# Recurrent stage of a hybrid decoder layer: the filler ordered between the first step's scores and its first inverse product, doubled

## The chip, the cores and the metric

One Trainium2 chip, of which the program uses one core. The metric is the device time of one execution in microseconds (us); of several runs the median stands. Five engines work side by side, each through its own queue in order: TensorE (PE in the profile; PEld is its weight loads), VectorE (DVE), ScalarE (ACT), GpSimd (POOL) and SyncE (SP, which here issues the DMAs). They wait for each other by semaphores.

## The reference

One layer over 2048 tokens of width 1024, all in float32: an RMSNorm, one input projection `p = h @ w_in` of 4224 columns, three branches on its columns, each with a SiLU gate, one output projection of the concatenated branches, the residual and a last RMSNorm.

- Branch A is differential attention: 4 heads, two causal softmax maps per head, `a = p0 - lam * p1`, and `a @ v`.
- Branch B is a short gated convolution of 256 channels.
- Branch C is the RWKV-7 recurrence, 4 heads of size 64. For each token

```
sa    = state @ kk_t
state = state * w_t - sa (kk_t * a_t)^T + v_t k_t^T
y_t   = state @ r_t
```

The kernel computes the recurrence in chunks of 64 tokens, which needs the inverse of a triangular 64x64 matrix for each chunk and head.

## The kernel before, in words

**Order of the work.** The 2048 tokens are two halves of 1024. A first stage projects what the recurrence of half 0 needs. Then four stages follow: `rwkv(0)`, `attention(0)`, `rwkv(1)`, `attention(1)` (lines 1420 to 1431), and at the end what is left of the filler. The order on TensorE is the order in which the program text issues its products; the other engines and the DMA queue are ordered by a scheduler that follows the program's order and an estimate of times.

**Filler.** All other products are one long list, the generator `filler` (line 1287): input projections of the convolution, of the attention heads and of half 1's recurrence, and at its end the output projection. An input projection (`inproj`, line 348) takes one weight tile of 128 columns through two chunks of 512 tokens, 24 products (line 357) per chunk, since float32 is done in three products of split operands. The weight tile is loaded by SP into one buffer (`fetch_w`, line 324) and split into a high and a low part by POOL (`load_w`, lines 341 and 343), with two buffers each. A chunk ends with its evacuation by ScalarE and DVE (lines 462 to 480 for the convolution, 374 to 408 for attention) and mostly a store. Between the two halves the list also rebuilds the normalized input (`stats`, line 224, and `make_h1`, line 305), while `attention(0)` runs.

The output projection comes as 16 output tiles of 48 products each (`out_tile`, line 1238; the product is line 1254). Tile i may start only when `state["allowed"]` is over i: it is 8 at first, and line 1428 raises it to 10, 12, 14 and 16 as the pairs of the last head of `attention(1)` are finished. If the next tile isn't allowed, `pull` (line 1318) gives nothing.

**How filler gets into a stage.** A stage is a generator too. Where it has issued something whose result takes a while, it yields a hint in microseconds, and `run` (line 1340) answers with filler until the hint is used up, at 0.216 per product (`T512`); hints are scaled by `SCALE`, 1.0 for `rwkv(0)` and 0.92 for `rwkv(1)`:

```
for f in gen:
    state["owed"] = max(state["owed"], -OWE) + f * scale
    while state["owed"] > 0:
        if not pull():
            state["owed"] = 0.0
            break
```

**The recurrent stage.** `rwkv(half)` (line 487) goes through a half in four steps of 256 tokens. A step has three parts. `early` (line 520) loads the projected rows, computes decay and gate inputs (the products of lines 533, 537, 564, 582 and 587, with a normalizing factor that goes through POOL at lines 572 and 577). `scores` (line 594) computes the chunk's score blocks (line 617), sends their triangular 16x16 blocks through DRAM into another layout (lines 638 and 640) and calls `inverse` (line 679), which inverts them on DVE (lines 693 and 696), stores them (`zd`, line 700) and loads them back as diagonal blocks (`Z`, line 703, eight DMAs). `late` (line 705) transposes these blocks on DVE (X, line 718), and its first product is the first inverse product, line 726; further inverse products and the state's update follow. After the first step's `early` and `scores` have been issued, each `late` is woven together with `early` and `scores` of the next step (lines 860 to 893). Line 870 stands once per half, between the first step's scores and its `late`:

```
for f in chain(0):
    if f != "free":
        yield f
yield WAIT[0]
for n in groups:
    lt, nx = late(st[n]), chain(n + 1)
```

**Attention.** A score unit is a pair of products (lines 1006 and 1007), a maximum on DVE (line 1012) and an exponential on ScalarE (line 1015); after each unit `attention` yields a hint (line 1191). Weighing (lines 1042 and 1052), transposes (line 1082), their copies (line 1087) and the products with V (line 1074) are spread between the units.

Of the kernel before, what the change touches and what calls it, by code (L numbers as in the profile page):

```python
# [61 lines left out]
LAG = 2  # L62
OSC = 1
PS = ((1, 0), (1, 1, 1, 1))
WAIT = (8.0, 15.0)
XH = 0.3
HC = 2.656
HG = 2.047
# [76 lines left out]
def trunk(ctx, tc, a, o, phases="RTO"):  # L145
# [341 lines left out]
    def rwkv(half, pool):  # L487
# [379 lines left out]
# [5 lines that stand above are left out]
# [15 lines left out]
            while more:  # L887
# [3 lines left out]
                elif x != "free":  # L891
                    yield x
            yield WAIT[1]

# [585 lines left out]
```

## Time and profile before

| what | value |
|---|---|
| time, median of 3 runs | 1620.57 us (1619.04 to 1622.68) |
| the profiled execution, its own time | 1626.87 us |
| its span, from the first instruction to the last | 1625.1 us |
| mean granted clock of TensorE in it | 0.965 of full speed |
| busy: PE, DVE, ACT, POOL | 93%, 55%, 44%, 40% of the span |
| TensorE instructions | 10328 |

All rows of the profile come from one execution, so they are to be read against its own time. A row of the timeline gives the start in us from the span's start, the duration, engine, line and operation, what is written and read, the number of equal instructions merged in it, and in brackets the idle time of the engine just before it and the instruction that ended it. Products are pipelined: each is shown for about 0.4 us, while the next starts 0.23 us later. The granted clock is 1.00 at 2.4 GHz and 0.50 at 1.2 GHz, and a mean between the two in a stretch that has both.

### The profile page before, as it was taken

The numbers are of one execution on the slowest core, as the hardware profiler recorded it, in microseconds if no ns is written. First come the engines' busy times: TensorE is split into PE (matmuls) and PEld (weight loads), VectorE is DVE, ScalarE is ACT, GpSimd is POOL, SyncE is SP. The second block draws the span as 40 slices with busy tenths as digits, with TensorE's granted clock in tenths as the row PEclk, the third lists the DMA queues.
The fourth block names the chain that finished last, engine by engine and source line by source line (L and its number), as shares of the span: only waits on it lengthen the run. The fifth ranks groups of instructions, "written<-read, shape, count | busy, mean of one in ns | idle before, by whom it ended". The sixth has DMA issues, their size and how long they took to land.

```text
span 1625.1 us, 28369 instructions
## 1 busy us (share of the span) xinstructions
PE 1512.6 (93%) x10328; PEld 1224.4 (75%) x10328; DVE 891.0 (55%) x1987; ACT 720.3 (44%) x1751; POOL 649.1 (40%) x898
## 2 busy tenths in 40 slices
PE   5999899999997879999989999999899999988998
PEld 4777677878786657888867878788678878766886
DVE  7553555554215766862545565427757756775611
ACT  6432121222126555652212212127668777776732
POOL 4675334352325543434432434333534323111343
PEclk9999899999999989999979999999999999988999
DMA  6324212233376543323323222263544243321233
GB/s 220 104 91 160 67 33 80 73 102 100 116 246 203 149 145 117 103 73 128 112 72 101 74 56 61 70 220 97 152 129 157 93 143 100 95 77 40 67 111 110
DMA packets 140620, 180.76 MB, mean 111 GB/s; under 512 B 34336, under 2 KB 85568, under 8 KB 140480
## 3 DMA queue, kind: packets, MB, share of 16 engines
q1 hardware_dynamic: 140480, 178.94, 35.3%
q8 instruction: 82, 1.34, 0.4%
q14 instruction: 58, 0.48, 0.1%
HBM read 125.40 MB, written 53.48 MB: 110 GB/s over the span
## 4 chain that ended last, share of the span: by engine, by line
PE 71%; DVE 8%; issue 4%; DMA 3%; ACT 3%; POOL 3%; SPq 1%; POOLq 0%; DVEq 0%; ACTq 0%
PE pj L357 33%; PE ops L1254 10%; PE av L1074 7%; PE aT L1082 4%; PE S L1006 3%; PE S L1007 3%; DVE nm L1012 1%; DVE P L1052 1%; ACT P L1042 1%; ACT P L1015 1%; DVE tmpx L693 1%; PE G L617 1%; PE wu L770 1%; POOL wl L343 1%; PE chp L814 1%
## 5 line engine op out<-in xcount | busy, mean ns | idle before, releaser
L357 PE MATMUL pj<-hh,wh 128*128 128x512 f32 x1008 | 414.1, 411 | 7.9 <-DVE tlo L394 3.8
L357 PE MATMUL pj<-hh,wl 128*128 128x512 f32 x1008 | 412.9, 410 | 0.1
L357 PE MATMUL pj<-hl,wh 128*128 128x512 f32 x1008 | 409.9, 407 | 0.0
L343 POOL TENSOR_TENSOR wl<-wr,wh 128x256 fp32r<-128x256 f32 x324 | 261.6, 837 | 46.7 <-ACT wh L338 43.5
L1015 ACT ACTIVATE P<-S,nm 128x512 f32<-128x512 f32 (+3 forms) x320 | 199.5, 625 | 99.9 <-DVE nm L1012 89.2
L1012 DVE TENSOR_REDUCE nm<-S 128x1 f32<-128x512 f32 (+3 forms) x320 | 192.8, 607 | 88.8 <-PE S L1007 84.5
L357 PEld LDWEIGHTS pj<-hh,wh 128*128 128x128 f32 x1008 | 192.5, 191 | 50.5 <-issue 10.3
L357 PEld LDWEIGHTS pj<-hh,wl 128*128 128x128 f32 x1008 | 192.4, 191 | 42.8 <-issue 3.3
L357 PEld LDWEIGHTS pj<-hl,wh 128*128 128x128 f32 x1008 | 192.8, 191 | 38.9 <-issue 1.4
L341 POOL TENSOR_SCALAR wh<-wr 128x512 fp32r<-128x512 f32 x132 | 83.6, 650 | 272.3 <-PE pj L357 202.7
L1006 PE MATMUL S<-K,QH 128*128 128x512 f32 (+2 forms) x320 | 129.6, 405 | 31.8 <-ACT P L1015 31.6
L1074 PE MATMUL av<-aTf,V 128*128 128x256 f32 x576 | 152.8, 390 | 0.5 <-ACT aTf L1087 0.5
L1007 PE MATMUL S<-K,QL 128*128 128x512 f32 (+2 forms) x320 | 120.5, 377 | 0.0
L1052 DVE SCALAR_TENSOR_TENSOR P<-P,sc 128x512 f32<-128x512 f32 (+3 forms) x160 | 112.1, 735 | 13.2 <-ACT P L1042 9.5
L1074 PEld LDWEIGHTS av<-aTf,V 128*128 128x128 f32 x576 | 104.3, 196 | 12.2 <-ACT aTf L1087 1.1
L1254 PE MATMUL ops<-woh,wh 128*128 128x512 f32 x256 | 105.6, 413 | 5.6 <-ACT wh L1233 5.6
L1087 ACT COPY aTf<-aT 128x512 f32<-128x512 f32 x144 | 83.5, 584 | 56.7 <-PE aT L1082 55.9
L1254 PE MATMUL ops<-wol,wh 128*128 128x512 f32 x256 | 106.0, 414 | 0.0
L1254 PE MATMUL ops<-woh,wl 128*128 128x512 f32 x256 | 105.9, 414 | 0.0
L1011 DVE TENSOR_TENSOR S<-S,bt 128x256 f32<-128x256 f32 (+1 forms) x152 | 57.6, 379 | 84.1 <-PE S L1007 78.2
L1006 PEld LDWEIGHTS S<-K,QH 128*128 128x128 f32 x320 | 62.9, 196 | 53.2 <-ACT P L1015 40.4
L1082 PE MATMUL aT<-con,P 128*128 128x128 f32 x576 | 92.2, 285 | 11.3 <-DVE P L1052 8.3
(289 smaller groups left out, 2323.9 us busy)
## 6 DMA issues: line engine op xcount, KB each, us to landing
wr<-in_wt_dram SPq DMA_DIRECT2D x81, 512.0 KB, 3.8
wr<-mx SPq DMA_DIRECT2D x128, 64.0 KB, 2.0
oxt<-in_x_dram SPq DMA_DIRECT2D x32, 256.0 KB, 3.1
out_dram<-oxt SPq DMA_DIRECT2D x32, 256.0 KB, 2.4
prw<-s SPq DMA_DIRECT2D x28, 256.0 KB, 2.0
V<-pv SPq DMA_DIRECT2D x24, 256.0 KB, 2.9
x<-in_xT_dram SPq DMA_DIRECT2D x16, 256.0 KB, 6.3
pv<-t SPq DMA_DIRECT2D x16, 256.0 KB, 2.3
```

The lines of the kernel that those rows point to most:

```text
L341: nc.gpsimd.tensor_scalar(wh[:, ks], wr[:, ks], 1.0, 1.0, ALU.mult, ALU.mult)
L343: nc.gpsimd.tensor_tensor(wl[:, ks], wr[:, ks], wh[:, ks].bitcast(F32), ALU.subtract)
L357: mm(ps, lhs[:, k], rhs[c][k], start=(n == 0), stop=(n == 3 * NK - 1))
L1006: mm(s[:, 0:sw], QH[:, m, off:off + P], K[:, m, 0:sw], start=True, stop=False)
L1007: mm(s[:, 0:sw], QL[:, m, off:off + P], K[:, m, 0:sw], start=False, stop=True)
L1012: nc.vector.tensor_reduce(nm[:, m, g:g + 1], s[:, 0:gw], AX.X, ALU.max, negate=True)
L1015: act(p[:, 0:gw], s[:, 0:gw], AF.Exp, bias=nm[:, m, g:g + 1], accum_out=l[:, m, g:g + 1])
L1052: stt(pt[1, g][:, 0:gw], pt[1, g][:, 0:gw], sc[:, 1, g:g + 1], pt[0, g][:, 0:gw], ALU.mult, ALU.add)
L1074: mm(av[:, 0:256], Vs.get((h, kc))[:, ko:ko + P], tf[:, d * 256:d * 256 + 256], start=kb + d == 0, stop=kb + d == nb - 1)
L1082: nc.tensor.transpose(t[:, d * 256 + qi * P:d * 256 + qi * P + P], x["A"][g][:, ko:ko + P], ident)
L1087: cpy(tf, t)
L1254: mm(ps, l[:, k], Ws[n][r][k], start=(c == 0), stop=(c == 3 * NK - 1))
```

## The change

The first of the two values of `WAIT` is 16 in place of 8. It is read at line 870 alone, once in `rwkv(0)` and once in `rwkv(1)`; the second value (line 893, after each step's `late`) stays. No instruction is added or taken away.

```diff
 LAG = 2
 OSC = 1
 PS = ((1, 0), (1, 1, 1, 1))
-WAIT = (8.0, 15.0)
+WAIT = (16.0, 15.0)
 XH = 0.3
 HC = 2.656
 HG = 2.047
```

## Rows read from the trace of the kernel before

**Rows 1.** The page: busy time, share of the span and instructions of the engines.

```profile
PE 1512.6 (93%) x10328; PEld 1224.4 (75%) x10328; DVE 891.0 (55%) x1987; ACT 720.3 (44%) x1751; POOL 649.1 (40%) x898
```

**Rows 2.** What TensorE waited for, whole span: us in total, times, longest.

```profile
PE S L1006 <- ACT P L1015: 31.6, 17, 6.6
PE p L726 <- DVE X L718: 16.0, 3, 7.9
```

**Rows 3.** Timeline of TensorE at the first step of half 0.

```profile
190.76 0.39 PE L357 MATMUL pj<-hh,wh 128*128 128x512 f32 x1
190.99 0.40 PE L357 MATMUL pj<-hl,wh 128*128 128x512 f32 x1
199.30 1.05 PE L726 MATMUL p<-X,N 32*32 32x16 f32 x64 [7.91 <-DVE X L718]
...
211.72 0.95 PE L564 MATMUL ssp<-conr,e 128*128 128x2 f32 x8
```

**Rows 4.** Timeline of TensorE at the first step of half 1.

```profile
812.09 0.40 PE L357 MATMUL pj<-hh,wl 128*128 128x512 f32 x1
819.69 1.05 PE L726 MATMUL p<-X,N 32*32 32x16 f32 x64 [7.20 <-DVE X L718]
...
832.25 0.95 PE L564 MATMUL ssp<-conr,e 128*128 128x2 f32 x8
```

**Rows 5.** Stretches: length, busy per engine (instructions), granted clock, DMA share, GB/s.

```profile
199.30:204.00 4.70, 4.70 (x72) 3.08 (x72) 1.05 (x3) 0.84 (x2) 0.00 (x0) 0.50 0.43 152
...
208.00:212.00 4.00, 4.00 (x76) 3.36 (x74) 2.95 (x6) 0.73 (x2) 1.87 (x2) 0.65 0.19 66
212.00:216.00 4.00, 4.00 (x50) 3.19 (x51) 0.46 (x2) 0.95 (x2) 2.42 (x3) 1.00 0.02 4
```

**Rows 6.** Timeline of TensorE at the second step of half 0.

```profile
269.21 0.72 PE L726 MATMUL p<-X,N 32*32 32x16 f32 x64 [0.94 <-DVE X L718]
...
276.74 0.95 PE L564 MATMUL ssp<-conr,e 128*128 128x2 f32 x8
...
284.39 0.81 PE L582 MATMUL bcp<-con,e__2679 128*128 128x128 f32 x4 [2.29 <-POOL e__2679 L577]
```

**Rows 7.** Timeline of all engines between inverse and X, half 0.

```profile
192.17 0.32 SPq L700 DMA_DIRECT2D zd<-Zs  x1
...
193.00 0.69 DVE L479 SCALAR_TENSOR_TENSOR th<-th,pj 128x512 f32<-128x512 f32 x1 [1.32 <-ACT th L478]
193.71 3.63 SPq L703 DMA_DIRECT2D Z<-zd  x8
...
198.71 0.45 DVE L718 STREAM_TRANSPOSE X<-Z 128x256 f32<-128x256 f32 x1 [5.02 <-DMA Z<-zd]
```

**Rows 8.** Timeline of POOL: casts of the next weight tile, half 0 and half 1.

```profile
179.30 2.82 POOL L343 TENSOR_TENSOR wl<-wr,wh 128x256 fp32r<-128x256 f32 x4
...
798.01 2.82 POOL L343 TENSOR_TENSOR wl<-wr,wh 128x256 fp32r<-128x256 f32 x4
```

**Rows 9.** Line 1254 alone by stretches: length, TensorE busy (products), clock, DMA share, GB/s.

```profile
1230.00:1414.50 184.50, 109.17 (x372) 1.00 0.35 109
1414.50:1491.00 76.50, 0.48 (x1) 0.89 0.23 68
...
1574.60:1618.00 43.40, 43.40 (x189) 1.00 0.37 119
```

**Rows 10.** ScalarE by line, from 1230 to 1414.5 and from 1414.5 to 1491.

```profile
L1015 ACT ACTIVATE P<-S,nm 128x512 f32<-128x512 f32 (+3 forms) x90 | 57.8, 642 | 22.8 <-DVE nm L1012 21.2 <-DVE ors L1112 1.0
...
L1015 ACT ACTIVATE P<-S,nm 128x512 f32<-128x512 f32 (+3 forms) x46 | 29.8, 649 | 5.4 <-DVE nm L1012 5.0 <-DVE mn L1026 0.3
```

**Rows 11.** Stretches before and in the hold, columns as in rows 5.

```profile
1384.00:1414.50 30.50, 30.50 (x155) 25.66 (x153) 21.63 (x54) 21.04 (x55) 6.42 (x10) 1.00 0.19 59
1414.50:1491.00 76.50, 64.46 (x311) 52.54 (x309) 56.15 (x140) 61.93 (x158) 8.55 (x14) 0.89 0.23 68
```

**Rows 12.** Timeline of POOL ahead of line 582, second step of half 0.

```profile
282.19 1.65 POOL L572 TENSOR_TENSOR rn<-ssb,mexp 128x8 f32<-128x8 f32 x1
```

**Rows 13.** The stretch of the input's rebuilding in the first attention, columns as in rows 5.

```profile
480.00:630.00 150.00, 120.92 (x549) 97.02 (x548) 102.10 (x242) 86.50 (x235) 71.10 (x98) 0.91 0.54 167
```

## Prediction
> **What bounds the kernel now.** I read the page's shares first: TensorE is busy for 1512.6 us of the 1625.1 us span [rows 1], in an order of its own written out by the program, so time is lost where it stands idle or runs slowly. The list of what TensorE waits for comes next [rows 2]. Two lines lead it. One is spread over attention (17 waits for the exponentials of ScalarE); the other, 16.0 us in three waits, is the first inverse product (line 726) waiting for the transposed blocks X (line 718), which is the place that the change touches.
>
> The timeline shows two of these three waits to be the first step of each half. In half 0 the last filler product before it starts at 190.99 us; products follow each other at 0.23 us, so TensorE is free at 191.22, and the inverse product starts at 199.30 after an idle time of 7.91 us [rows 3]. In half 1 the same happens from 812.09 to 819.69, with 7.20 us idle [rows 4]. The stall costs more than itself: behind half 0's the granted clock is 0.50, the 1.2 GHz level, still 0.65 in the mean from 208 to 212 us, and 1.00 (2.4 GHz) from 212 [rows 5]. What that costs can be read by comparison. From the inverse product to the product of line 564 the program issues the same list in each of these steps, filler included. Half 0's first step needs 211.72 - 199.30 = 12.42 us for it, half 1's 832.25 - 819.69 = 12.56 us, and half 0's second step, which came from a wait of only 0.94 us and was not slowed, 276.74 - 269.21 = 7.53 us [rows 3, 4, 6]. So the low clock costs 4.9 and 5.0 us.
>
> **The change, part by part.** It raises one hint from 8 to 16. A hint is turned into filler at 0.216 per product and is scaled by 1.0 in half 0 and by 0.92 in half 1: 8 / 0.216 = 37 more products before the first inverse product of half 0, 7.36 / 0.216 = 34 in half 1. Nothing is added or removed in the kernel; 71 products with what hangs on them come earlier.
>
> *At the stall.* 37 x 0.23 = 8.5 us end at 191.22 + 8.5 = 199.7, 34 x 0.23 = 7.8 us end at 812.32 + 7.8 = 820.1. X would have let TensorE go at 199.30 and 819.69, so each inverse product starts 0.4 us later than now, without an idle time ahead of it, and what follows runs at the 2.4 GHz level: 0.4 - 4.9 = -4.5 us and 0.4 - 5.0 = -4.6 us, together **-9.1 us** by the end of the second recurrence, with 71 products done that are still to come in the kernel before.
>
> Does X come as it does now? Its chain is DVE, ScalarE, a store (192.17), eight loads on SP (from 193.71, 3.63 us) and the transpose at 198.71 [rows 7]; none of it hangs on filler. The 37 and 34 products are less than one weight tile of 48, whose weights POOL had cast by 182.1 and 800.8 us [rows 8]; in half 0 a tile had just ended. The casts of the tile after that come from one tile further on, beside the stall in both kernels. The new filler ends one 24-product group in front of X; its evacuation (one ScalarE and one DVE operation, DVE's like the 0.69 us of the one at 193.00 [rows 7]) can come between the loads and X on DVE, which I bound at 0 to 0.7 us in each half and take at 0, since X is only needed at the end of the filler. SP gets one store of 256 KB at most, behind the eight loads in program order. I put it at nothing; if it slipped ahead it would cost one issue, by the eight loads 3.63 / 8 = 0.45 us.
>
> *Where the 71 products are missing.* Not in the last stretch. The filler ends in output tiles of 48 products, and the program lets only tiles 0 to 7 go before the last head's first pair is finished. In the trace these 8 x 48 run out at 1414.5 us; between 1414.5 and 1491 there is one such product in the record, and attention goes on bare [rows 9]. Tile 8 starts with that pair in both kernels, so the 189 products of the pure tail stay. What changes is that the bare stretch begins 71 products earlier. With filler, 184.5 us carry 90 score units, 2.05 us each with 372 / 90 = 4.1 products; bare, 76.5 us carry 46, 1.66 us each [rows 9, 10]. 71 / 4.1 = 17 units become bare, at 2.05 - 1.66 = 0.39 us: **-6.7 us**. The bounds are from the same rows. Above: a unit costs as much bare as filled, 0. Below: all of their 71 x 0.23 = 16.3 us comes off. In the 30.5 us before the hold TensorE is busy throughout and ScalarE for 21.0 us [rows 11], so the lower bound would need ScalarE to do nearly all of that in 14.2 us; the hold's mean is the nearest row.
>
> The clock is where a rule speaks against this part. The hold has a granted clock of 0.89 where the stretches before have 1.00 [rows 11]. The Trainium skill, "TensorE: Matmul & The Clock Gate", section "A second HAM failure mode: psum-queue depth-cycling", says that short idle times between groups of products can keep the clock swinging between its levels, so that throughput falls without any one long wait; by it a longer bare stretch would be worth nothing, and the sum would be -9.1 us. The trace agrees as far as 0.89 goes, and the 1.66 us already hold it.
>
> **The sum** is -9.1 - 6.7 = -15.8 us. In the profiled execution's own time, 1626.87 us, that is 1611.1; that execution lies 6.3 us above the median of 1620.57, against which I state it: 1620.57 - 15.8 = **1604.8 us**.
>
> **The rivals.**
> (a) The hold takes all of it back: -9.1 us, 1611.5. For it speaks its low clock, against it the 1.66 us.
> (b) The 71 products come off whole: -9.1 - 16.3 = -25.4 us, 1595.2. Against it ScalarE's 21.0 us.
> (c) The filler meets other work. Every later transfer of the filler falls 37 or 71 products earlier against recurrence and attention. A weight cast or a gating product on POOL just ahead of the chain to line 582 is such a meeting: in the second step it held POOL until 282.19, and TensorE waited 2.29 us [rows 6, 12]. More is at stake in the first attention, where the filler rebuilds the normalized input for half 1: 480 to 630 us holds 150 - 120.9 = 29.1 us of idle time at a clock of 0.91 [rows 13]. If that grew by half, 14.5 us, the result would be -1.3 us, 1619.3; it can as well shrink. From about 19 us more it would be slower.
> (d) Slower: X slides behind the new filler. If the inverse chain, its loads or the transpose were ordered after the added evacuations, on DVE or SP, the old wait would stand behind 8.5 and 7.8 us of more filler, with the low clock behind it: +16.3 - 6.7 = +9.6 us, 1630.2. With the low clock back the front is at +0.8 plus the new waits, so with the hold's 6.7 us it decides from 5.9 us of new waits over both halves. Against it: SP issues the loads 1.2 us after the store, with no filler's transfer between [rows 7].
> (e) The hints do nothing (the filler held or used up): 1620.6. The filler isn't held before the output tiles, so this is nearly excluded.
>
> **How the numbers follow.** Forecast 0.58, with a range of its own from 1599 to 1611 (collisions on POOL and shifts in the handover, each a few us either way); (a) 0.16; (b) 0.08; (c) 0.11; (d) 0.05; (e) 0.02. A measurement of this kernel can tell about 0.2%, 3.2 us, from no change. Faster: 0.58 + 0.16 + 0.08 and 0.04 of (c) = 0.86. Same: 0.06 of (c) and (e) = 0.08. Slower: (d) and 0.01 of (c) = 0.06. The range reaches to (b) below and past (a) above, to 1616, which takes in 4.5 us of collisions beside (a); outside are (d), (e) and most of (c).
>
> **What would show it.** Right: the two long waits of line 726 for X gone, or under 1 us; the granted clock 1.00 through both first steps; from the inverse product to line 564 some 7.5 us in each; the second recurrence's end about 9 us earlier with 71 products more behind it; the last output product before the hold about 17 x 2.05 + 9.1 = 44 us earlier than 1414.5, the hold some 17 units longer, and as many products in the pure tail. Wrong: a wait of over 3 us left at line 726, a hold whose units cost 2 us, or an idle time between 480 and 630 us that differs from 29 us by more than 8.

## The result, and the profile after

| what | before | after |
|---|---|---|
| median (lowest to highest) of 4 runs, us | 1620.46 (1619.04 to 1622.68) | 1604.62 (1603.98 to 1606.58) |
| ratio, 95% interval | | 0.9892, [0.9870, 0.9914] |
| profiled execution: own time, span, us | 1626.87, 1625.1 | 1604.13, 1601.9 |
| mean granted clock | 0.965 | 0.977 |

The changed kernel is 15.8 us faster. The page's first part answers to [rows 1]: TensorE is busy for 12 us less, and its share of the span goes up from 93 to 94%.

```profile
PE 1500.6 (94%) x10328; PEld 1213.6 (76%) x10328; DVE 894.2 (56%) x1987; ACT 722.1 (45%) x1751; POOL 645.9 (40%) x898
```

The list of TensorE's waits over the whole span (us in total, times, longest) answers to [rows 2]. The wait for X has gone from 16.0 us to 3.2, and second stands a projection's product (line 357) that waits 8.1 us in one piece.

```profile
PE S L1006 <- ACT P L1015: 30.2, 19, 5.2
PE pj L357 <- DVE tlo L394: 8.1, 1, 8.1
...
PE p L726 <- DVE X L718: 3.2, 3, 1.5
```

The timeline of TensorE shows the two places of [rows 3, 4] (start, duration, in brackets the idle time ahead and who ended it), between them the product that waits 8.15 us, and last the end of the stretch without filler, the first product of output tile 8.

```profile
200.24 0.73 PE L726 MATMUL p<-X,N 32*32 32x16 f32 x64
...
207.78 0.95 PE L564 MATMUL ssp<-conr,e 128*128 128x2 f32 x8
...
477.46 0.77 PE L357 MATMUL pj<-hh,wh 128*128 128x512 f32 x1 [8.15 <-DVE tlo L394]
...
814.95 0.72 PE L726 MATMUL p<-X,N 32*32 32x16 f32 x64 [1.51 <-DVE X L718]
...
822.24 0.95 PE L564 MATMUL ssp<-conr,e 128*128 128x2 f32 x8
...
1472.03 0.80 PE L1254 MATMUL ops<-woh,wh 128*128 128x512 f32 x1 [5.73 <-ACT wh L1233]
```

The wait at 477.46 is not new as such. The same product (1440 of line 357 go before it in both kernels) waits in the kernel before too, but less, and later. There 1406 of these products stand ahead of the first attention's first score, so it falls inside attention. The change puts 1443 ahead of that score, and the wait moves in front of attention. Timeline of the kernel before, whose first score is at 478.5 us:

```profile
494.63 0.76 PE L357 MATMUL pj<-hh,wh 128*128 128x512 f32 x1 [3.79 <-DVE tlo L394]
```

In half 0 there is no wait left for X, and line 564 follows 7.54 us behind the inverse product; in half 1 a wait of 1.51 us is left, and it is 7.29 us. Before it was 12.42 and 12.56. The stretches (columns as in [rows 5]) say why: the clock behind the inverse product is 1.00 where it was 0.50.

```profile
200.20:204.00 3.80, 3.77 (x76) 2.45 (x75) 1.38 (x3) 0.84 (x2) 0.00 (x0) 1.00 0.55 197
815.00:819.00 4.00, 3.96 (x76) 2.68 (x77) 1.68 (x3) 0.84 (x2) 0.00 (x0) 1.00 0.51 184
1370.00:1471.00 101.00, 81.37 (x396) 64.68 (x394) 75.23 (x189) 80.28 (x209) 11.63 (x19) 0.92 0.20 59
480.00:630.00 150.00, 124.82 (x593) 102.10 (x593) 108.17 (x255) 84.58 (x226) 73.56 (x101) 0.92 0.47 148
```

The third of these lines is the bare stretch, which answers to [rows 11]. From its last output product (1369.38 us) to the next one (1472.03) it is 102.6 us long, where the kernel before has 80.5 us in its profile and 77.1 in a second one (run e6 below). ScalarE's line for it (as [rows 10]) holds 62 score units, 16 more than before:

```profile
L1015 ACT ACTIVATE P<-S,nm 128x512 f32<-128x512 f32 (+3 forms) x62 | 40.1, 649 | 9.8 <-DVE nm L1012 9.3 <-DVE mn L1026 0.3
```

**Where the time went, by stage.** I cut each kernel's TensorE timeline at the same instructions: the first score block of a half (line 617), line 564 of its first step, line 833 of its fourth step, and the first and last scores of attention (line 1006). "Handover" is from a recurrence's fourth step to the first attention score. Since the profiled execution of before lay 6.3 us above the median, the kernel before was profiled a second time (the run e6 below, 1620.91 us). The two differ mainly in the first attention, 234.1 against 228.2 us. I take that for scatter between executions. The differences in this text go by the second profile, and each other stage time comes from one profile too, so a few us in the first attention say little.

| stage, us | before | before, second | after | difference |
|---|---|---|---|---|
| first step, half 0 | 43.7 | 44.6 | 39.4 | -5.2 |
| steps 2 to 4 | 214.2 | 213.3 | 209.4 | -3.9 |
| handover | 52.6 | 52.5 | 61.7 | +9.2 |
| attention, half 0 | 234.1 | 228.2 | 226.9 | -1.3 |
| first step, half 1 | 42.2 | 42.2 | 38.9 | -3.3 |
| steps 2 to 4 | 203.0 | 203.0 | 202.3 | -0.7 |
| handover | 48.6 | 48.6 | 50.6 | +2.0 |
| attention, half 1, up to the last tiles | 411.3 | 411.2 | 396.9 | -14.3 |
| last tiles | 122.7 | 122.5 | 122.6 | +0.1 |

What is not in the table differs by 0.3 us at most. The spans differ by -17.2 us, against -15.8 by the medians.

### The profile page after: what moved, and what is told of

Same layout as the page of the kernel before. It is cut to its first block, busy times and chain, and to the rows that moved or that the text cites. A ratio compares the mean times of both kernels' runs of the same rounds, so it can differ in the third digit from the quotient of the medians.

```text
span 1601.9 us, 28378 instructions
## 1 busy us (share of the span) xinstructions
PE 1500.6 (94%) x10328; PEld 1213.6 (76%) x10328; DVE 894.2 (56%) x1987; ACT 722.1 (45%) x1751; POOL 645.9 (40%) x898
## 4 chain that ended last, share of the span: by engine, by line
PE 68%; DVE 8%; DMA 5%; ACT 4%; issue 3%; SPq 3%; POOL 2%; DVEq 0%; POOLq 0%; ACTq 0%
PE pj L357 31%; PE ops L1254 10%; PE av L1074 7%; PE S L1006 3%; PE aT L1082 3%; PE S L1007 3%; ACT P L1042 1%; ACT P L1015 1%; DVE nm L1012 1%; PE wu L770 1%; PE G L617 1%; DMA wr<-in_wt_dram 1%; POOL wl L343 1%; DMA xt<-in_x_dram 1%; DVE P L1052 1%
## 5 line engine op out<-in xcount | busy, mean ns | idle before, releaser
L357 PE MATMUL pj<-hh,wl 128*128 128x512 f32 x1008 | 407.4, 404 | 0.6 <-POOL wl L343 0.5
L1082 PE MATMUL aT<-con,P 128*128 128x128 f32 x576 | 91.4, 283 | 14.9 <-DVE P L1052 7.8
```

The costliest lines, as they stand in the source:

```text
L357: mm(ps, lhs[:, k], rhs[c][k], start=(n == 0), stop=(n == 3 * NK - 1))
L1082: nc.tensor.transpose(t[:, d * 256 + qi * P:d * 256 + qi * P + P], x["A"][g][:, ko:ko + P], ident)
```

## The experiments

None of these kernels leaves out any part of the computation; they only order the same work differently. Edits are against the changed kernel. Each was compared with the kernel before on its own chip, and the ratios are to that.

### One half at a time

`e1_half0`:

```diff
-        yield WAIT[0]
+        yield (16.0, 8.0)[half]
```

> 16 in half 0, 8 kept in half 1. Theory (cover): the wait of line 726 in half 0 is gone and its low clock with it (-4.5 us), and 37 products fewer stand beside the second attention ahead of the hold (9 units bare, at 0.39 to 0.65 us: -3.5 to -5.9): 1610 to 1613 us, half 1's wait of 7 us unchanged. Rival (handover): what half 0 gains is taken back where half 1's input is rebuilt, as the new wait of 8.1 us for tlo at 477 us of the changed kernel suggests: within 3 us of the kernel before.

Measured: 1609.63 us, ratio 0.9932 [0.9911, 0.9953]. Its timeline:

```profile
200.79 0.72 PE L726 MATMUL p<-X,N 32*32 32x16 f32 x64
...
476.38 0.77 PE L357 MATMUL pj<-hh,wh 128*128 128x512 f32 x1 [6.67 <-DVE tlo L394]
...
812.33 1.05 PE L726 MATMUL p<-X,N 32*32 32x16 f32 x64 [8.90 <-DVE X L718]
```

`e2_half1`:

```diff
-        yield WAIT[0]
+        yield (8.0, 16.0)[half]
```

> 8 in half 0, 16 in half 1. Theory (cover): half 0's wait of 7.9 us stays, half 1's goes with its low clock (-3.3 to -4.6 us, since X came 1.5 us late in the changed kernel), and 34 products fewer ahead of the hold (-3.2 to -5.3): 1611 to 1614 us, and both halves alone add up to the whole change. Rival (handover takes half 0's share back): nearly the whole gain is here, 1605 to 1608.

Measured: 1620.77 us, 0.9986 [0.9967, 1.0005]. Its timeline in half 1:

```profile
813.28 0.73 PE L726 MATMUL p<-X,N 32*32 32x16 f32 x64 [0.56 <-DVE X L718]
...
820.60 0.95 PE L564 MATMUL ssp<-conr,e 128*128 128x2 f32 x8
```

Each half's wait goes with its own hint, and only with that: 5.1 us less in the first step of half 0 in e1, 4.0 us less in that of half 1 in e2. The wait in the first handover comes with half 0's hint. Half 0's part is worth 0.7%. Half 1's part alone gives no measurable gain, against the 1611 to 1614 us that was expected, so the two do not add up to the whole. In e2's profile what the front wins is lost in the same half: steps 2 to 4 take 206.9 us for 203.0. Of that 1.4 us is idle time (with new waits of 2.47 us at line 357 and 1.44 us at line 582), the rest busy time of TensorE at a granted clock of 0.98 for 0.99.

### The same filler, but not earlier as a whole

`e3_moved_within` gives 8 us back behind the last step, so the front is filled and no product leaves attention for the recurrence:

```diff
-            yield WAIT[1]
+            yield WAIT[1] - (8.0 if n == len(groups) - 1 else 0.0)
```

> 16 at the first step and 8 less after the last step of each half, so that the 71 products come from within the stage and the hold begins where it did before. Theory (cover): 15.1 us of waits and 9.9 us of low clock come off, less 0.8 us, and the 71 products removed elsewhere are off a busy TensorE: -24 us, 1596, about 8 us faster than the changed kernel. Rival (handover): with 8 us less between the stages the second half's input and the attention's first loads come too late, and 5 to 10 us are given back there: 1602 to 1608.

Measured: 1598.86 us, 0.9863 [0.9841, 0.9885], which is lower than the changed kernel's 0.9892, though the two intervals overlap. Its profiled execution (1593.87 us) is 5.0 us below its median. The fronts are as in the changed kernel (39.4 and 38.0 us). The second attention takes 410.8 us up to the last tiles, as before. What it wins beside the front is in the handovers, 43.9 and 40.8 us for 52.5 and 48.6, for the filler that is taken out there; the first attention is 3.6 us longer (231.8 us for 228.2), which is within the scatter seen above.

`e5_late_only` is the opposite: the kernel before, with the 8 us added behind the last step.

```diff
-WAIT = (16.0, 15.0)
+WAIT = (8.0, 15.0)
...
-            yield WAIT[1]
+            yield WAIT[1] + (8.0 if n == len(groups) - 1 else 0.0)
```

> 8 kept at the first step, and 8 more after the last step of each half: the same 71 products earlier, but not where the stall is. Theory (cover): both waits of line 726 and the low clock stay; 16.3 us of products more in the stages, of which the hold gives back 6.7 (by the prediction) to 10.4 us (by the two traces): 6 to 10 us slower than the kernel before, 1626 to 1630. Rival (position): the gain comes from the filler being ahead, whatever it covers: faster than before, 1605 to 1615.

Measured: 1619.24 us, 0.9982 [0.9968, 0.9996], between the two ranges expected. Both waits and the low clock behind them stay:

```profile
200.58 1.05 PE L726 MATMUL p<-X,N 32*32 32x16 f32 x64 [7.82 <-DVE X L718]
...
825.34 1.05 PE L726 MATMUL p<-X,N 32*32 32x16 f32 x64 [8.93 <-DVE X L718]
...
836.72 0.95 PE L564 MATMUL ssp<-conr,e 128*128 128x2 f32 x8
```

Against the second profile of before, the handovers grow by 14.3 and 8.3 us and the first attention shrinks by 5.6. The second attention up to the last tiles shrinks by 16.5 us, as it does by 14.3 us in the changed kernel. Sending these 71 products ahead of attention is worth about 15 us there, whichever hint sends them; the place where they are put then decides whether that is kept.

### More, and less, of it

`e4_24` and `e7_12` change the one number (24.0 and 12.0 for 16.0 in line 65).

> 24 in place of 16: another 37 and 34 products with no wait left to cover. Theory (stall covered at 16, products ahead of the hold come off at nearly their own price, as the late-only run showed): 16.3 us more in the stages, 14 to 19 us less in the second attention, so within 4 us of the changed kernel, 1601 to 1609, no wait at line 726. The prediction's own sizing of the hold (6.7 us back for 71 products): 9.6 us slower than the changed kernel, 1614.

Measured: 1619.70 us, 0.9986 [0.9975, 0.9997], above both values expected.

> 12: 18 and 17 products more than before, 4.2 and 3.9 us of the two waits. Theory: waits of 3 to 4 us are left and the clock falls to the 1.2 GHz level behind them too, so the front gains little (an idle time replaced by work of the same length) and only half of the products' way through the hold shows: 1614 to 1621. Rival (the clock's cost goes with the idle time): half of the whole gain, 1611 to 1614.

Measured: 1607.38 us, 0.9911 [0.9893, 0.9928]. 

At 24 the filler outlasts X, and the first step takes 48.0 us in half 0 (39.4 in the changed kernel) and 45.8 in half 1 (38.9). The second attention up to the last tiles takes 392.6 us for 396.9: the next 71 products bring only 4.3 us there, where the first 71 brought 14.3. The first handover is 74.4 us. There TensorE waits three times for a weight tile that POOL casts (timeline):

```profile
460.70 0.50 PE L357 MATMUL pj<-hh,wh 128*128 128x512 f32 x1 [3.98 <-POOL wh L341]
...
473.96 0.79 PE L357 MATMUL pj<-hh,wh 128*128 128x512 f32 x1 [5.41 <-POOL wh L341]
...
486.06 0.80 PE L357 MATMUL pj<-hh,wh 128*128 128x512 f32 x1 [4.07 <-POOL wh L341]
```

At 12 about half of each wait is filled, and the other half is left. The timeline, and a stretch behind the first wait:

```profile
199.59 1.05 PE L726 MATMUL p<-X,N 32*32 32x16 f32 x64 [3.63 <-DVE X L718]
...
212.25 0.95 PE L564 MATMUL ssp<-conr,e 128*128 128x2 f32 x8
...
804.74 1.05 PE L726 MATMUL p<-X,N 32*32 32x16 f32 x64 [4.62 <-DVE X L718]
```

```profile
199.60:204.00 4.40, 4.40 (x71) 3.26 (x72) 0.78 (x2) 1.32 (x3) 0.00 (x0) 0.50 0.46 168
```

The clock falls all the same, and line 564 comes 12.7 us behind the inverse product, as in the kernel before. So in half 0 the first step gains only 0.7 us and in half 1 it loses 0.3. That part of the theory held: half the filler buys nothing at the front. And yet e7 takes 0.9% less time than the kernel before, less than either range expected. In its profile the gain stands elsewhere: steps 2 to 4 (-3.6 and -3.8 us), the first attention (-7.0) and the second (-3.2). Between 480 and 630 us its clock is 0.95 for 0.91. The -7.0 is hardly more than the 5.9 us by which two profiles of the kernel before differ in the first attention. None of these is a place that the hint fills, and why they gain is not shown.

### The kernel before, once more

> The kernel before once more, for a second profile. The profiled execution of before lies 6.3 us over its median, and its first attention is 6.2 us longer than in the run with 8 kept in half 0, where the program up to there is the same. If that is scatter of the executions, this profile has its first attention at 226 to 230 us and the rest of its stages within 2 us of the first profile; if not, 234 again.

Measured (one execution): 1620.91 us, span 1619.1. The first attention takes 228.2 us, which is what was expected if the 234.1 of the first profile are scatter. It shows the wait ahead of line 582 (first of the lists of TensorE's waits below, 205 to 427 us) and, in the second attention (1078 to 1490 us), a longest wait for the exponentials of 6.3 us. The timeline puts that one near the attention's start, where the weights of the output projection are set up:

```profile
PE bcp L582 <- POOL e__2679 L577: 2.3, 1, 2.3
...
PE S L1006 <- ACT P L1015: 18.9, 11, 6.3
```

```profile
1172.13 0.80 PE L1006 MATMUL S<-K,QH 128*128 128x512 f32 x1 [6.31 <-ACT P L1015]
```

The changed kernel's list for the same part of the second attention has no wait over 3.3 us:

```profile
PE S L1006 <- ACT P L1015: 19.3, 15, 3.3
```

The long wait is there wherever the second attention has the filler of before (6.55 us in the first profile, 6.31 here, 7.17 in e3) and the first output product comes 69 units into attention. No wait for the exponentials ahead of that product is over 1.7 us in the changed kernel, e1, e2, e5 and e7, where it comes after 52 to 61 units.

### Spreading what is left: a version that beats both

If the bare stretch is what attention loses, less filler per score unit earlier on should leave some for it. `e8_spread` is e3 with one more number:

```diff
-UNIT = (1.0, 0.894)
+UNIT = (1.0, 0.7)
...
-            yield WAIT[1]
+            yield WAIT[1] - (8.0 if n == len(groups) - 1 else 0.0)
```

> The run moved within the stage (16 first, 8 less after the last step), and 0.7 in place of 0.894 as the hint of a unit of the second attention, so that the filler before the hold reaches to its end. Theory: the hold's 19 us of idle time and some 8 us of low clock go, less what the longer units lose elsewhere: 12 to 25 us faster than the run moved within the stage, 1574 to 1587. Rival (ScalarE and DVE set the pace of the attention either way, and the filler left over is added to the tail): within 5 us of it.

Measured: 1587.49 us, 0.9784 [0.9761, 0.9807], the fastest of all: 34 us below the kernel before by their medians, some 13 us below e3 (0.9784 against 0.9863). The two profiled executions differ by only 3.5 us, since e8's lies 2.9 us above its median and e3's 5.0 below. The stretches of its second attention:

```profile
1057.30:1256.00 198.70, 185.38 (x924) 152.97 (x923) 151.90 (x337) 150.66 (x375) 74.34 (x99) 0.99 0.44 138
1256.00:1515.00 259.00, 246.31 (x1227) 203.79 (x1226) 162.75 (x391) 185.32 (x455) 72.16 (x107) 0.97 0.31 93
```

TensorE is busy for 95% in the second, up to and past the end of attention, where the bare stretch had 81% in the changed kernel and a clock of 0.92. From the first score to the last output product it takes 523.9 us; e3 took 533.6. Half 1's first step gives 3.2 us of that back (41.2 us for 38.0), behind a fall of the clock that the last section shows.

### Taking the new wait of the handover apart

At the wait in the handover (477.46) the trace shows ScalarE squaring rows of the next half's input (line 232) as their loads land, with the filler's evacuation (line 393, then line 394 on DVE) in its queue behind them. Timeline of the changed kernel:

```profile
472.61 0.63 ACT L232 ACTIVATE xt<-xt 128x512 f32<-128x512 f32 x1 [2.27 <-DMA xt<-in_x_dram]
...
475.38 0.60 ACT L393 ACTIVATE thi<-pj 128x512 fp32r<-128x512 f32 x1
...
476.62 0.69 DVE L394 SCALAR_TENSOR_TENSOR tlo<-pj,thi 128x512 fp32r<-128x512 f32 x1 [1.89 <-ACT xt L232]
```

`e9_stats_spread` hands these squares out one by one: after every 11 filler products of the attention projection ahead, it issues one square and the load of the next (line numbers behind line 231 are one higher in its profile):

```diff
-    def stats(c):
+    def stats(c, out):
...
+                yield
                 act(xt, xt, AF.Square, accum_out=ss[:, i, j:j + 1])
...
-        return rs
+        out.append(rs)
...
-            yield from each(*att_steps(0, h))
-        rs = [stats(c) for c in range(2)]
+            g = (s for c in range(2) for s in stats(c, rs)) if h == 2 else iter(())
+            for n, x in enumerate(each(*att_steps(0, h))):
+                yield x
+                if n % 11 == 10:
+                    next(g, None)
+            for _ in g:
+                pass
```

> The changed kernel, with the 16 loads and squares of the second half's sum of squares (lines 231 and 232) issued one by one between the projections of the head before, in place of all at once. Theory: in the changed kernel the in-order ScalarE works off 16 squares that wait for their loads, in front of the evacuation that TensorE's next product needs (8.15 us at line 394); spread out, that wait goes, and the stretch from the last step to the first score falls from 61.6 to 53 us: 5 to 9 us faster than the changed kernel, 1596 to 1600. Rival (the first loads of the attention, on the same queue, hold the evacuation's buffers): the wait stays and the time is within 3 us of the changed kernel.

Measured: 1604.57 us, 0.9889 [0.9846, 0.9931]: no gain over the changed kernel's 0.9892. The handover takes 65.5 us for 61.7, and the first attention 223.5 for 226.9. (Half 1's first step is also 4.5 us longer, with a clock of 0.50 from 820 to 824 us behind a wait of 1.60 us for X.) The wait at line 394 is gone, and two others stand in its place:

```profile
440.80 0.73 PE L407 MATMUL vp<-con,t 128*128 128x128 f32 x4 [3.42 <-ACT t L402]
...
473.28 0.79 PE L358 MATMUL pj<-hh,wh 128*128 128x512 f32 x1 [3.94 <-POOL wh L342]
```

But e9 did not take the squares out of the way. Its first wait ends with the copy of line 402, and that copy stands in ScalarE's queue right behind a square that has waited 3.72 us for its load:

```profile
439.55 0.63 ACT L233 ACTIVATE xt<-xt 128x512 f32<-128x512 f32 x1 [3.72 <-DMA xt<-in_x_dram]
...
440.18 0.57 ACT L402 COPY t<-pj 128x512 f32<-128x512 f32 x1
```

`e10_both` is e8 and e9 together.

> The run spread over the second attention, with the same spread of the loads and squares. Theory: its wait of 4.5 us at line 394 goes with its low clock: 4 to 8 us faster than that run, 1580 to 1584. Rival: the wait is hidden or replaced in the first attention, which is held up by other waits anyway: within 3 us of it.

Measured: 1593.59 us, 0.9828 [0.9792, 0.9865], so rather slower than e8; its first handover takes 55.7 us for 44.0. A wait of 8.1 us is there again, in the list of waits of 425 to 480 us, though the squares are spread out:

```profile
PE pj L358 <- DVE tlo L395: 8.1, 1, 8.1
```

Here too squares stand ahead of the evacuation (line 394, at 455.09 us) and wait for their loads, the last of them for 2.62 us (timeline):

```profile
454.46 0.63 ACT L233 ACTIVATE xt<-xt 128x512 f32<-128x512 f32 x1 [2.62 <-DMA xt<-in_x_dram]
```

So these two runs show that this way of spreading brings nothing. They don't refute the theory of the squares' place, since evacuations still waited behind squares, and the squares for their loads. What the trace adds is the load on the DMA engines in the handover. The stretches of the changed kernel, DMA share and GB/s last:

```profile
450.00:470.00 20.00, 19.31 (x84) 15.27 (x82) 1.38 (x2) 5.74 (x15) 7.97 (x12) 1.00 0.95 296
470.00:480.00 10.00, 2.54 (x7) 2.20 (x8) 2.48 (x6) 7.21 (x22) 4.92 (x7) 0.71 0.89 291
```

In e4 (450 to 470 us) it is 0.89. In the first profile of before it is 0.79 from 450 to 478.5 us, and TensorE doesn't idle there. A handover limited by its transfers fits e4, where the weights are late, and e9 and e10, where squares and a weight tile wait for their loads. Against it speaks that the share alone doesn't tell the one from the other: in the changed kernel TensorE is busy for 19.31 of 20 us at 0.95, and in e3's handover it doesn't idle at 0.88:

```profile
440.00:461.30 21.30, 21.30 (x94) 17.34 (x93) 2.76 (x4) 2.40 (x4) 4.41 (x7) 1.00 0.88 264
```

No run took transfers out of the handover. What is shown is where its 9 us are (8.15 us of them in the one wait) and that this wait stands there where the product comes ahead of the first score. The same wait has 6.67 us in e1 and 4.76 in e5, ahead of the first score too, and inside attention 3.8 and 2.9 us in the kernel before, 5.9 in e3 and e7. **What sets its length stays open**.

## Why the prediction was right, and where it was not

The forecast was 1604.8 us, and 1604.62 was measured. The number is right partly by luck, because its errors cancel.

**The front: right.** Forecast -9.1 us, measured -5.2 and -3.3, together -8.5. The long waits are gone, the clock behind them is 1.00, and lines 726 to 564 take 7.54 and 7.29 us where 7.5 was forecast. e1 and e2 show that each half's part hangs on its own hint. The part is mainly the clock's and not the wait's, as the prediction had it: e7 fills half of the wait and gets nothing.

**X taken as unmoved: right in half 0, 2 us late in half 1.** The inverse product of half 1 starts 31.6 us behind the first score block where it started 29.4 us behind (second profile). The delay is there already at the store ahead of X: 806.66 us in the second profile of before (score blocks at 784.3), 807.72 after (783.3), so 2.1 us lie ahead of the store, and the way from there to X is 6.56 and 6.64 us. "None of it hangs on filler" did not hold: on DVE two evacuations of the filler (798.27 us, 0.68 us; 801.95, 0.69) stand among the inversion's instructions in the changed kernel, and one (801.54, 0.68) in the second profile of before. In e2, where half 0's filler comes as before, the inversion starts on DVE 14.9 us behind the score block, as in the second profile of before; in the changed kernel it is 16.6. The front of half 1 got 3.3 us for the 4.6 forecast. One more DVE evacuation, 0.69 us, does fall between the loads and X, as the prediction had bounded it; it cost next to nothing.

```profile
807.72 0.32 SPq L700 DMA_DIRECT2D zd<-Zs  x1
...
812.95 0.69 DVE L394 SCALAR_TENSOR_TENSOR tlo<-pj,thi 128x512 fp32r<-128x512 f32 x1 [4.86 <-DMA Z<-zd]
...
814.36 0.45 DVE L718 STREAM_TRANSPOSE X<-Z 128x256 f32<-128x256 f32 x1 [0.72 <-DMA Z<-zd]
```

**The hold: the mechanism right, the term mis-sized.** Forecast -6.7 us (17 units at 0.39), measured -14.3. What was to be seen is there: 62 units for 46, the last product before the hold at 1369.4 us, 45 earlier than 1414.6 (44 forecast), 102.6 / 62 = 1.66 us per bare unit, and the same tail. The step that failed is "17 units become bare, at 2.05 - 1.66 = 0.39 us". It priced both ends by the means of two stretches, and the bare one was read to 1491 us only, 4 us ahead of the hold's end (1495.1). The hold grew by 25.5 us, where 17 x 1.66 = 28.2 was forecast. The part with filler shrank by 39.8 us, where 17 x 2.05 = 34.9 was forecast: by 48.1 ahead of the first output product, which now comes after 52 units and not 69 (141.0 to 92.9 us), less 8.3 that the part from there to the hold grew.

The two stretches from the first score to the hold's end, of the second profile of before and of the changed kernel, say the same in terms of TensorE (length, then busy time):

```profile
1078.10:1489.31 411.21, 381.19 (x1879) 316.23 (x1877) 281.66 (x659) 298.94 (x744) 124.67 (x175) 0.97 0.35 110
1075.10:1472.03 396.93, 366.07 (x1804) 301.30 (x1803) 280.37 (x657) 296.24 (x741) 117.71 (x169) 0.97 0.35 108
```

The forecast let 16.3 us of products go and gave 16.3 - 6.7 = 9.6 us back as idle time. Measured, TensorE is busy for 15.1 us less, and its idle time is 30.9 us for 30.0. In the hold it did grow, by 4.8 us (15.9 to 20.7), and by 3.8 from the first output product to the hold (3.8 to 7.6); but ahead of the first output product it fell by 7.8 (10.4 to 2.6), 6.3 of which are the one wait at the setup of the output weights. The clock of that first part went from 0.94 (0.98 in the first profile) to 1.00. e5 shows the term without the front: -16.5 us for the same 71 products. It isn't in proportion: with 34 products moved (e2) it is -2.2 us, with 37 (e1) -6.9, with none (e3) -0.4, with 142 (e4) -18.6. That first part loses its idle time in e1, e2 and e7 as well (2.6 to 2.8 us are left), so the lost wait alone doesn't make the 14.3; their holds have a clock of 0.89, 0.85 and 0.84, the changed kernel's 0.91. What sets the size stays open.

**The handover: the mis-size's counterweight, and rival (c) in part.** The prediction took its sum to be complete with two terms and left this to a rival, as idle time between 480 and 630 us. That idle time went from 29.1 to 150 - 124.8 = 25.2 us, which shows nothing (the second profile of before has 25.1). The meeting is just ahead of that window: 8.15 us at 477.46, at the product that waited 3.8 us inside the window before. The handover costs 9.2 us, and the attention behind it gives 1.3 back. The other meeting that (c) named, POOL ahead of line 582 in the second step, went the good way: the 2.3 us wait is gone from the list of waits of 205 to 420 us (the 0.2 us that stands there for line 582 is at 213.34 us, in the first step), and a new one of 1.4 us at line 617 is smaller. Steps 2 to 4 gained 3.9 us.

```profile
PE G L617 <- DVE DE L631: 1.4, 1, 1.4
...
PE bcp L582 <- POOL e__1972 L577: 0.2, 1, 0.2
```

In all: -8.5 for the front, -14.3 in the hold's attention, +9.2 - 1.3 + 2.0 at the handovers, -3.9 - 0.7 in later steps. The two terms that the prediction had come to -22.8, 7 us more than forecast, and what it had left at nothing to +5.3.

**The rivals.** (a), the hold takes all back, falls: it gave 14.3, and the longer hold's clock, 0.91, lies between the 0.89 and 0.93 of the two profiles of before. (b), the 71 products come off whole, is the nearer one for that term alone (-16.3), but for the time it is 9 us too low. (d) falls: X is 2 us late in half 1, but doesn't slide behind the filler at 16, and the clock stays at 1.00. At 24 it is the filler that outlasts X, another way to the same loss. (e) falls. (c) came true in part: filler met other work at another place than it named, for some 8 us of its 14.5, and the time is not the one it gave.

## What to carry to other kernels

Filling a wait in part can buy nothing at that place (e7): where a low clock follows the wait, look at the granted clock behind it. Filler brought forward is missing somewhere, and what it is worth there is not the difference of two stretches' means; look at the idle time of all the parts that shift, single long waits above all, and at which product of the filler comes to stand ahead of the next stage. Where filler runs out early, rationing it is a second gain: e8 takes 0.8% off e3 by one number, 0.894 to 0.7, where placing it gave 1.1 to 1.4%.

## What was not expected of the hardware

The price of the low clock did not go with the length of the wait: lines 726 to 564 take 12.4 us behind 7.91 us, 12.7 behind 3.63. And the clock fell behind waits that are shorter than others behind which it did not. In e8 it follows a wait of 0.76 us in half 1, and 10.1 us go by to line 564 (timeline and stretch); in the changed kernel 1.51 us at the same place are followed by 1.00 and 7.3 us.

```profile
802.94 0.73 PE L726 MATMUL p<-X,N 32*32 32x16 f32 x64 [0.76 <-DVE X L718]
...
813.08 0.95 PE L564 MATMUL ssp<-conr,e 128*128 128x2 f32 x8
```

```profile
806.00:810.00 4.00, 4.00 (x32) 2.33 (x35) 2.55 (x5) 1.81 (x5) 0.00 (x0) 0.50 0.12 33
```

So the length of the one wait doesn't decide; what does, these runs leave open.
